# Pairs of attention heads, scan outputs and states packed side by side on the array, with later modulation products

## The chip, the cores and the metric

The kernel runs on one core of one Trainium2 chip. The metric is the device time of one execution in microseconds (us). In the profile, PE is TensorE's matmul, PEld its weight load, DVE is VectorE, ACT is ScalarE, POOL is GpSimd, SP is SyncE, which issues most of the transfers.

## What is computed

A block with two layers over 512 latent tokens of 1024 features, and 256 context tokens that only layer 0 reads. Layer 0 has one input projection; its columns feed attention (8 query heads of 64, 2 key/value heads, per-head RMSNorm, rotary positions on the latent tokens) and a bidirectional state-space scan (8 heads of 64, 2 groups, state 64, chunks of 128 tokens). Both results go through one output projection. Layer 1 is a gated short convolution. A SwiGLU feed-forward follows each layer, and shift, scale and gate vectors ("modulation") come from a conditioning vector times `ada_w`.

```python
def attend_blocks(q, keys, vals):
...
        s = jnp.einsum('bqkgd,bskd->bkgqs', qi, keys).astype(jnp.float32) * scale
        pr = jax.nn.softmax(s, axis=-1).astype(vals.dtype)
        return jnp.einsum('bkgqs,bskd->bqkgd', pr, vals)
...
    states = jnp.einsum('bclgn,bgecl,bclgep->bcgepn', bc, decay_to_end, xdt)
...
    y_off = jnp.einsum('bclgn,bgecl,cbgepn->bclgep', cc, jnp.exp(a_cs), h_in)
    y = (y_diag + y_off).reshape(b, t, nh, p)
...
        mod = (jax.nn.silu(c) @ ada_w[i] + ada_b[i])[:, None, :]
...
        x = x + g1 * m_lat
```

## The kernel before

Activations lie with features on the 128 partitions. Large projections are made of three fp32r matmuls (`mm3`: high by high, high by low, low by high part). The attention values, the scan's states and outputs and most small matmuls are plain fp32, which TensorE takes as two records each in the trace.

**Order.** Instructions are written by Python generators, and a scheduler orders each engine's queue by a simulated time line; inside `manual_schedule` PE's written order is kept. `run` calls `hybrid`, then the output projection (`project`, with a lead of three output blocks that leave out the last attention pair), the feed-forward and layer 1.

**The stretch that the change touches** is `mixer`. It projects keys, values and `dt` for six chunks, then queries, then ten blocks of features (`feature`), of which blocks 0 to 5 are convolved and 6 to 9 are the scan's gate. `heads_prep` and `rope` normalize and rotate queries and keys. The rotated query `qd` is written twice side by side (64 + 64 columns), so that one transpose of 128 columns puts the query on both halves of the partitions. `to_tok` turns features into tokens; `btok` holds each group's B twice for the same reason. `ssd_context` and `ssd` run the scan: `ssd_states` weights the tokens on POOL (`xw`) and multiplies them with the doubled B, `ssd_advance` adds the result to the running states `hin`, and `ssd_unit` (eight: four chunks by two groups) builds decay exponents (`lp`, `ep`), `cb`, and the outputs `yp`, in which one matmul of 128 weight columns covers two heads and half of the product is not used.

**Attention** goes head by head. `attn_prep` transposes the queries, finds each row's maximum with a DVE reduction over 768 scores (`mx`, line 804) and a diagonal (`dm`, line 805), and puts it into the query tile. `attn_head` makes scores (line 822), exponents on ACT (`ex`, line 824) and values (line 830): `vz` holds 64 columns of ones beside the values, so the 128 output rows are 64 values and 64 copies of the row sum. After each second head a DVE chain (lines 882 to 887) normalizes the pair.

**The interleaving** is in `mixer`: each round advances the scan one step, attention one step, and from the second round on the queue `ada` by three steps. That queue (`ada_rest`) computes three modulation vectors of layer 0 (among them the gate of the output projection): 24 loads of 256 columns by 2 through the weight ring `wst` (three buffers, shared with `take`'s prefetched weights), each followed by two DVE multiply-adds of 128 x 512 (line 257), and a transpose and reduction for each eighth product.

PSUM is dealt as three buffers of one bank (`psA`), one of one bank (`psV`), and two of two banks (`psS`).

Of the kernel before, what the change touches and what calls it, by code (L numbers as in the profile page):

```python
# [7 lines left out]
F32 = mybir.dt.float32  # L8
# [28 lines left out]
CON = {"ident": (0, 0), "ones": (0, 128), "fold": (0, 256), "pick": (0, 384), "tri_le": (1, 0), "tri_ge": (1, 128),  # L37
       "cos": (2, 0), "sin": (2, 128)}
CAT = (0, 388, 644, 900)
# [19 lines left out]
class Block:  # L59
# [328 lines left out]
    def mixer(self, mp, h, hc, hcp):  # L388
        nc, tc, t = self.nc, self.tc, self.t
        kt = [mp.tile([P, 768], F32R, name=f"kt{g}") for g in range(2)]  # L390
        vz = mp.tile([P, CHUNKS, 2, 192], F32, name="vz")
        nc.gpsimd.memset(vz, 1.0)
        dt = mp.tile([P, CHUNKS, 16], F32, name="dt")
        qd = mp.tile([P, 4, 8, 2, 64], F32, name="qd")
# [24 lines left out]
        qn = qd[:, :, :, 0, :]  # L419
        for c in range(CHUNKS):  # L420
# [5 lines left out]
            nc.vector.tensor_copy(vz[:, c, :, 64:128], kv[c][:, 128:256].rearrange("p (a b) -> p a b", a=2))  # L426
# [24 lines left out]
        btok = sm.tile([P, CHUNKS, 2, 2, 64], F32, name="btok")  # L451
# [100 lines left out]
    def rope(self, pool, dst, src, tab, nh):  # L552
# [25 lines left out]
    def to_tok(self, j, src, c0, nc_, xtok, btok):  # L578
# [8 lines left out]
        else:  # L587
            s = tp.rearrange("p c (g n) -> p c g n", g=2)
            for c in range(nc_):
                nc.scalar.copy(btok[:, c0 + c], s[:, c, :, None, :].broadcast_to([P, 2, 2, 64]))  # L590
# [54 lines left out]
    def ssd_states(self, sp, sd, c, dirs, tag):  # L645
        nc = self.nc
        out = []
        for g in range(2):
            xw = sp.tile([P, 512], F32, name="xw", tag=tag, bufs=2).rearrange("p (a b c) -> p a b c", a=2, b=4)
            st = self.psA()  # L650
            for e in dirs:
# [3 lines left out]
            lo, n = 256 * dirs[0], 256 * len(dirs)  # L655
            nc.tensor.matmul(st[:, lo:lo + n], lhsT=sd["btok"][:, c, g].rearrange("p a b -> p (a b)"),
                             rhs=xw.rearrange("p a b c -> p (a b c)")[:, lo:lo + n], start=True, stop=True)
            for e in dirs:
                r = slice(64 * e, 64 * e + 64)
                out.append((g, e, st[r, 256 * e:256 * e + 256]))  # L660
# [17 lines left out]
    def ssd_context(self, pp, sd):  # L678
# [3 lines left out]
        st0 = self.ssd_states(pp, sd, 0, (0, 1), "cs_a512")  # L682
# [6 lines left out]
        st1 = self.ssd_states(pp, sd, 1, (0, 1), "cs_a512")  # L689
# [5 lines left out]
    def ssd(self, mp, sm, m, dt, xf, zf, bf, cf, sd, feature):  # L695
# [8 lines left out]
        def advance(a, b):  # L704
            for f, t, e in ((a, a + 1, 0), (b, b - 1, 1)):
# [436 lines left out]
```

## Time and profile before

| what | value |
| --- | --- |
| median of 3 runs | 1294.94 us (1293.56 to 1295.48) |
| profiled execution | 1294.68 us |
| its span | 1292.9 us |
| PE busy | 1241.5 us, 96% |
| PE weight loads busy | 1022.4 us, 79% |
| DVE busy | 731.7 us, 57% |
| ACT busy | 448.0 us, 35% |
| POOL busy | 182.7 us, 14% |

The shares are means over the whole program. The layer projections and feed-forwards fill most of it; `mixer`'s later part lies between about 145 and 331 us of the span. A matmul's record includes the time in which its results leave the array, so records overlap and their sum is more than the time in which columns stream.

### The profile page before, as it was taken

To read this page: it belongs to the slowest core of one execution; us is meant where nothing else is said; L and a number is where in the kernel's file an instruction comes from. 1 tells how busy PE (TensorE), PEld (TensorE's weight loads), DVE (VectorE), ACT (ScalarE), POOL (GpSimd) and SP (SyncE) were. 2 spreads that over 40 slices of the span, in tenths; PEclk is the share of its full clock that TensorE was granted. 3 is DMA by queue.
4 is the path that set the end of the run, shared out by engine and by line. 5 is a ranking of instruction groups with operands and counts; after the bars stand their busy time and mean duration, and the time that the engine had idled before them with its cause. 6 is when DMAs were issued, how large, how long until landed. Compare 5 with 4: busy or idle time off the path is not lost.

```text
span 1292.9 us, 15877 instructions
## 1 busy us (share of the span) xinstructions
PE 1241.5 (96%) x6086; PEld 1022.4 (79%) x6086; DVE 731.7 (57%) x1187; ACT 448.0 (35%) x675; POOL 182.7 (14%) x199
## 2 busy tenths in 40 slices
PE   5999988899999999999999999999999999999997
PEld 3887665567798888888888988888988888888886
DVE  4898899976464777788522564443643333332223
ACT  4534534455353222222222342223532222222221
POOL 3433435440220000000000110002200000000001
PEclk9998989999999999999999999999999999999998
DMA  9331453300413777777433323333133333333322
GB/s 370 125 98 49 123 166 119 98 1 1 149 63 122 229 250 241 226 235 255 123 102 90 115 67 97 98 98 114 50 114 98 98 98 98 92 96 90 92 88 66
DMA packets 54845, 158.52 MB, mean 123 GB/s; under 512 B 6000, under 2 KB 8688, under 8 KB 54512
## 3 DMA queue, kind: packets, MB, share of 16 engines
q1 hardware_dynamic: 54480, 157.20, 38.3%
q8 instruction: 48, 0.79, 0.3%
q10 hardware_dynamic: 288, 0.31, 0.1%
q14 instruction: 29, 0.24, 0.1%
HBM read 154.86 MB, written 2.10 MB: 121 GB/s over the span
## 4 chain that ended last, share of the span: by engine, by line
PE 83%; DVE 9%; issue 3%; DMA 3%; POOL 1%; ACT 1%; SPq 0%; DVEq 0%; ACTq 0%; POOLq 0%
PE psS L116 14%; PE psS L117 14%; PE psS L118 14%; PE psA L116 10%; PE psA L118 10%; PE psA L117 10%; PE psV L830 2%; DMA adaw<-ada 2%; PE psS L961 1%; DVE xtok L257 1%; DVE mx L804 1%; PE psS L822 1%; DVE wlo L95 1%; PE psS L963 1%; DMA xT<-xT 1%
## 5 line engine op out<-in xcount | busy, mean ns | idle before, releaser
L95 DVE TENSOR_TENSOR wlo<-wst,whi 128x1024 fp32r<-128x1024 f32 (+2 forms) x194 | 234.9, 1214 | 317.2 <-ACT whi L94 311.8
L94 ACT CAST whi<-wst 128x1024 fp32r<-128x1024 f32 (+2 forms) x194 | 198.4, 1026 | 549.9 <-PE psS L117 258.5
L116 PE MATMUL psS<-act_hi,whi 128*128 128x512 f32 x760 | 297.5, 391 | 1.0 <-DVE cs_a L573 0.9
L118 PE MATMUL psS<-act_hi,wlo 128*128 128x512 f32 x760 | 297.2, 391 | 0.0
L117 PE MATMUL psS<-act_lo,whi 128*128 128x512 f32 x760 | 297.2, 391 | 0.0
L118 PEld LDWEIGHTS psS<-act_hi,wlo 128*128 128x128 f32 x760 | 143.3, 189 | 30.0
L116 PEld LDWEIGHTS psS<-act_hi,whi 128*128 128x128 f32 x760 | 143.2, 188 | 29.3 <-issue 1.2
L117 PEld LDWEIGHTS psS<-act_lo,whi 128*128 128x128 f32 x760 | 143.2, 188 | 27.7
L325 POOL TENSOR_TENSOR sq_acc<-sq_acc,sq 128x512 f32<-128x512 f32 (+1 forms) x28 | 38.0, 1356 | 872.2 <-issue 645.7
L116 PE MATMUL psA<-ffn_h_hi,whi 128*128 128x512 f32 (+1 forms) x396 | 145.4, 367 | 0.0
L117 PE MATMUL psA<-ffn_h_lo,whi 128*128 128x512 f32 (+1 forms) x396 | 145.0, 366 | 0.0
L118 PE MATMUL psA<-ffn_h_hi,wlo 128*128 128x512 f32 (+1 forms) x396 | 145.0, 366 | 0.0
L257 DVE SCALAR_TENSOR_TENSOR ada_acc<-ada_st,silu_c,ada_acc 128x512 f32<-128x512 f32 x98 | 73.5, 750 | 25.5 <-DMA ada_st<-ada 24.0
L117 PEld LDWEIGHTS psA<-ffn_h_lo,whi 128*128 128x128 f32 x396 | 74.7, 189 | 12.0
L118 PEld LDWEIGHTS psA<-ffn_h_hi,wlo 128*128 128x128 f32 x396 | 74.7, 189 | 12.1
L116 PEld LDWEIGHTS psA<-ffn_h_hi,whi 128*128 128x128 f32 x396 | 74.7, 189 | 11.9
L116 PE MATMUL psA<-act_hi,whi 128*128 128x512 f32 (+1 forms) x216 | 80.0, 370 | 0.1
L118 PE MATMUL psA<-act_hi,wlo 128*128 128x512 f32 (+1 forms) x216 | 79.2, 367 | 0.8 <-DVE wlo L95 0.8
L117 PE MATMUL psA<-act_lo,whi 128*128 128x512 f32 (+1 forms) x216 | 79.6, 368 | 0.0
L916 DVE SCALAR_TENSOR_TENSOR xT<-psA,mod,xT 128x512 f32<-128x512 f32 (+1 forms) x40 | 25.6, 643 | 67.9 <-PE psA L118 67.7
L94 ACT CAST ffn_h_hi<-sg 128x512 fp32r<-128x512 f32 x44 | 27.3, 621 | 59.0 <-DVE sg L980 59.0
L118 PEld LDWEIGHTS psA<-act_hi,wlo 128*128 128x128 f32 x216 | 40.8, 189 | 8.1 <-DVE wlo L95 1.3
(297 smaller groups left out, 1810.7 us busy)
## 6 DMA issues: line engine op xcount, KB each, us to landing
wst<-w_gu SPq DMA_DIRECT2D x88, 512.0 KB, 3.6
ada_st<-ada SPq DMA_DIRECT2D x112, 256.0 KB, 4.0
wst<-w_dn SPq DMA_DIRECT2D x32, 512.0 KB, 3.5
wst<-ada SPq DMA_DIRECT2D x24, 512.0 KB, 3.8
wst<-w_sc SPq DMA_DIRECT2D x24, 512.0 KB, 3.7
adaw<-ada SPq DMA_DIRECT2D x16, 512.0 KB, 10.4
wst<-w_dn SPq DMA_DIRECT2D x16, 384.0 KB, 3.2
wst<-w_f SPq DMA_DIRECT2D x10, 512.0 KB, 3.6
```

Of the source, the lines that this page charges most:

```text
L94: nc.scalar.copy(hi, src)
L95: nc.vector.tensor_tensor(lo, src, hi.bitcast(F32), ALU.subtract)
L116: nc.tensor.matmul(out, lhsT=a[0], rhs=b[0], start=start, stop=False)
L117: nc.tensor.matmul(out, lhsT=a[0], rhs=b[1], start=False, stop=False)
L118: nc.tensor.matmul(out, lhsT=a[1], rhs=b[0], start=False, stop=stop)
L257: nc.vector.scalar_tensor_tensor(a, w[:, i], c, a, ALU.mult, ALU.add)
L325: nc.gpsimd.tensor_tensor(self.acc[:, ts], self.acc[:, ts], sq, ALU.add)
L804: nc.vector.tensor_reduce(mx[:, c:c + 1], s[:, 0:768], AX.X, ALU.max)
L822: nc.tensor.matmul(s[:, a * T:a * T + T], lhsT=kt[x][:, ks], rhs=q[x], start=(x == 0), stop=(x == 1))
L830: nc.tensor.matmul(av, lhsT=vz[:, kc, vs], rhs=e[:, a], start=(c + a == 0), stop=(c + a == CHUNKS - 1))
L916: nc.vector.scalar_tensor_tensor(xt[:, d, ts], ps, gate[:, d:d + 1], xt[:, d, ts], ALU.mult, ALU.add)
L961: nc.tensor.matmul(out, lhsT=a[:, k * P:(k + 1) * P], rhs=hi, start=(k == 0 and a is w[0]), stop=False)
```

## The change

Attention handles two heads of a key group together. The values are multiplied with 64 weight columns for each head, one head into partitions 0 to 63 of the output and the other into 64 to 127; row sums are separate matmuls with 32 columns of ones for each head and each half of the chunk pair, into four strips of 32 partitions of a `psA` tile. The partial sums are added by one more small matmul with a new constant `pair` after the transpose. Query tiles are turned with two fp32 matmuls of 64 columns each in place of a transpose of a doubled query; `qd`, `btok` and `vz` lose their doubled or constant parts. Scan outputs and states use halves of 64 columns for two heads or two directions, and the skip term of the scan runs on 128 partitions at once. Each set of such matmuls stands in `manual_schedule`, so nothing comes between. The tiles `q1` and `q2` get four buffers and `ex` four. The `ada` queue starts in the seventh round with two steps each.

```diff
-        vz = mp.tile([P, CHUNKS, 2, 192], F32, name="vz")
-        nc.gpsimd.memset(vz, 1.0)
+        vz = mp.tile([P, CHUNKS, 2, 64], F32, name="vz")
-        qd = mp.tile([P, 4, 8, 2, 64], F32, name="qd")
+        qd = mp.tile([P, 4, 8, 64], F32, name="qd")
...
-            if rounds:
-                self.pump(3, ada)
+            if rounds > 5:
+                self.pump(2, ada)
...
-        for (u, v), o, op in zip(uv, (0, 32), (ALU.subtract, ALU.add)):
+        for i, ((u, v), o, op) in enumerate(zip(uv, (0, 32), (ALU.subtract, ALU.add))):
+            if len(dst.shape) == 3:
+                (nc.vector, nc.gpsimd)[i].tensor_tensor(dst[:, :, o:o + 32], u, v, op)
+                continue
...
-            for c in range(nc_):
-                nc.scalar.copy(btok[:, c0 + c], s[:, c, :, None, :].broadcast_to([P, 2, 2, 64]))
+            nc.scalar.copy(btok[:, c0:c0 + nc_], tp.rearrange("p c (g n) -> p c g n", g=2))
...
-            nc.tensor.matmul(st[:, lo:lo + n], lhsT=sd["btok"][:, c, g].rearrange("p a b -> p (a b)"),
-                             rhs=xw.rearrange("p a b c -> p (a b c)")[:, lo:lo + n], start=True, stop=True)
+            with self.tc.manual_schedule(engines={mybir.EngineType.PE}):
+                for c, e in ends:
+                    nc.tensor.matmul(st[64 * e:64 * e + 64], lhsT=sd["btok"][:, c, g], rhs=xw[:, e], start=True, stop=True)
...
         def advance(a, b):
+            st = self.ssd_states(sp, sd, ((2 + a, 0), (2 + b, 1)), "da")
             for f, t, e in ((a, a + 1, 0), (b, b - 1, 1)):
-                self.ssd_advance(sd, hin[t], hin[f], self.ssd_states(sp, sd, 2 + f, (e,), "da"), 2 + f, e)
+                self.ssd_advance(sd, hin[t], hin[f], st, 2 + f, e)
...
-        yp = self.psA((P, 2, 2, P))
+        yp = self.psA((P, 2, P))
+        with self.tc.manual_schedule(engines={mybir.EngineType.PE}):
+            for j in range(2):
+                for w, x, first in ((xtok[:, cc], mt, True), (hin, ce, False)):
+                    for i in range(2):
+                        at = (2 * g + j) * P + 64 * i
+                        nc.tensor.matmul(yp[64 * i:64 * i + 64, j], lhsT=w[:, at:at + 64], rhs=x[:, 2 * j + i],
+                                         start=first, stop=not first)
         for j in range(2):
...
+            pr = 2 * g + j
+            nc.vector.scalar_tensor_tensor(y[:, pr, sl], xf[:, pr, sl], self.vec("d_skip", pr, 1), yp[:, j],
+                                           ALU.mult, ALU.add)
...
-        for c in range(4):
-            nc.tensor.transpose(out=tp[:, c], in_=qd[:, c, n].rearrange("p a b -> p (a b)"), identity=self.ident)
+        with self.tc.manual_schedule(engines={mybir.EngineType.PE}):
+            for c in range(4):
+                for e in range(2):
+                    nc.tensor.matmul(tp[64 * e:64 * e + 64, c], lhsT=qd[:, c, n], rhs=self.ident, start=True, stop=True)
...
+    def attn_pair(self, ap, qs, kt, vz, u):
...
+        av, sm = self.psV(), self.psA()
...
+        def values(c):
+            e = [es.pop((h, c)) for h in range(2)]
+            first, last = c == 0, c == CHUNKS - 2
+            with self.tc.manual_schedule(engines={mybir.EngineType.PE}):
+                for a in range(2):
+                    kc = c + a + 2 if c < 4 else c + a - 4
+                    for h in (1, 0):
+                        nc.tensor.matmul(av[64 * h:64 * h + 64], lhsT=vz[:, kc], rhs=e[h][:, a], start=first and a == 0,
+                                         stop=last and a == 1)
+                for h in (1, 0):
+                    for a in range(2):
+                        r = 64 * h + 32 * a
+                        nc.tensor.matmul(sm[r:r + 32], lhsT=self.con("ones", 32), rhs=e[h][:, a], start=first, stop=last)
...
+        for c in range(0, CHUNKS, 2):
+            scores(0, c)
+            yield
+            scores(1, c)
+            yield
+            if c:
+                values(c - 2)
+                yield
+        values(CHUNKS - 2)
+        nc.scalar.copy(u[1], sm)
+        nc.scalar.copy(u[0], av)
...
+            nc.vector.transpose(flat, u[1])
+            tot = self.psA((P, 16))
+            nc.tensor.matmul(tot, lhsT=self.con("pair"), rhs=rt[:, :, 0], start=True, stop=True)
...
+            nc.vector.reciprocal(rs, tot)
```

## Rows read from the trace of the kernel before

**Rows 1.** Windows: us, then each engine's busy us (instructions), PEclk, DMA share, GB/s.

```profile
90.00:105.00 15.00, 11.90 (x57) 9.93 (x56) 15.00 (x21) 3.67 (x7) 13.36 (x14) 0.81 0.15 39
145.00:165.00 20.00, 17.07 (x66) 11.44 (x66) 19.02 (x29) 6.25 (x10) 13.27 (x15) 1.00 0.61 175
165.00:180.00 15.00, 12.31 (x40) 8.61 (x39) 13.07 (x20) 6.37 (x12) 7.25 (x11) 0.77 0.49 156
...
195.00:255.00 60.00, 50.79 (x182) 31.75 (x181) 57.75 (x86) 25.41 (x43) 31.84 (x26) 0.97 0.36 115
255.00:300.00 45.00, 41.61 (x165) 28.34 (x165) 35.12 (x71) 23.64 (x41) 15.99 (x15) 1.00 0.00 1
300.00:331.00 31.00, 31.00 (x142) 22.53 (x141) 14.01 (x28) 14.80 (x23) 0.00 (x0) 1.00 0.00 1
```

**Rows 2.** Waits, 145 to 331 us: total us, times, longest.

```profile
ACT dm L805 <- DVE mx L804: 36.5, 22, 5.9
```

**Rows 3.** Chain that ended last, 160 to 172 us: start, us, what.

```profile
162.51 3.64 DMA wst<-w_o
...
167.77 0.88 ACT dm L805 x3
```

**Rows 4.** Timeline of SyncE's queue, 138 to 190 us: start, us, instruction.

```profile
152.25 7.59 SPq L251 DMA_DIRECT2D wst<-ada  x3
```

**Rows 5.** Chain that ended last, 296 to 345 us.

```profile
297.07 0.44 PE psA L791 x4
297.51 0.43 PE psA L779 x2
...
298.38 1.72 PE psV L830 x4
...
305.22 0.92 PE psS L822 x4
...
339.21 1.23 DVE wlo L95
```

**Rows 6.** PE groups by form, 145 to 331 us: xcount, busy, mean ns.

```profile
L830 PE MATMUL psV<-ex,vz 128*128 128x512 f32 x96 | 46.8, 611 | 0.0
...
L779 PE MATMUL psA<-lx,xtok 128*128 128x256 f32 x32 | 10.1, 399 | 3.5 <-DVE xf L784 1.8 <-DVE q L795 0.9 <-DVE lx L774 0.8
L780 PE MATMUL psA<-ce,hin 128*128 128x256 f32 x32 | 9.5, 379 | 0.0
...
L656 PE MATMUL psA<-xw,btok 128*128 128x256 f32 x24 | 8.1, 447 | 0.9 <-DVE zf L479 0.5 <-POOL xw L652 0.4
...
L791 PE MATMUL psA<-cons,qd 128*128 128x128 f32 x32 | 5.2, 291 | 0.0
L656 PE MATMUL psA<-xw,btok 128*128 128x512 f32 x8 | 4.5, 641 | 2.8 <-POOL xw L652 1.8 <-ACT btok L590 1.0
```

**Rows 7.** PE timeline of `strips`, starts up to 34.19, then up to 34.40 us.

```profile
33.98 0.42 PE L203 MATMUL psS<-adaw,silu_w 128*32 128x256 f32 x4 [1.28 <-issue]
...
33.98 0.64 PE L203 MATMUL psS<-adaw,silu_w 128*32 128x256 f32 x8 [1.28 <-issue]
```

**Rows 8.** Timeline around line 761, 216.0 to 218.6 us.

```profile
216.54 0.52 PE L802 MATMUL psS<-kt,q 128*128 128x512 f32 x2
216.99 0.30 PEld L761 LDWEIGHTS psA<-cf,bf 64*128 64x128 f32 x2 [0.25 <-issue]
...
217.40 0.19 PEld L758 LDWEIGHTS psA<-da,band 128*128 128x128 f32 x1
```

**Rows 9.** DVE groups, 195 to 255 us.

```profile
L257 DVE SCALAR_TENSOR_TENSOR xtok<-wst,silu_c,xtok 128x512 f32<-128x512 f32 x20 | 22.7, 1136 | 0.3
```

**Rows 10.** DVE groups by form, 145 to 331 us.

```profile
L784 DVE SCALAR_TENSOR_TENSOR xf<-xf,vecs,psA 64x128 f32<-64x128 f32 x32 | 11.0, 343 | 10.0 <-PE psA L780 9.7
```

**Rows 11.** DVE and POOL groups by form, 80 to 106 us.

```profile
L565 DVE TENSOR_TENSOR qd<-rp_u,rp_v 128x256 f32<-128x256 f32 x8 | 4.3, 564 | 0.0
...
L565 POOL TENSOR_TENSOR qd<-rp_u,rp_v 128x256 f32<-128x256 f32 x8 | 7.8, 990 | 1.8 <-DVE rp_v L561 1.8
```

More of the change, by code (lines that the diff above doesn't have):

```diff
@@ L36 @@
 NROW = 160
-CON = {"ident": (0, 0), "ones": (0, 128), "fold": (0, 256), "pick": (0, 384), "tri_le": (1, 0), "tri_ge": (1, 128),
+CON = {"ident": (0, 0), "ones": (0, 128), "fold": (0, 256), "pick": (0, 384), "pair": (0, 388), "tri_le": (1, 0), "tri_ge": (1, 128),
        "cos": (2, 0), "sin": (2, 128)}
-CAT = (0, 388, 644, 900)
+CAT = (0, 516, 772, 1028)
 NCON = CAT[-1]
@@ L418, in mixer @@
         kn = pp.tile([P, CHUNKS, 2, 64], F32, name="kn")
-        qn = qd[:, :, :, 0, :]
+        qn = qd
         for c in range(CHUNKS):
@@ L643, in ssd_masks, with ssd_states @@
         sd.update(tri=tri, band=band)
-    def ssd_states(self, sp, sd, c, dirs, tag):
+    def ssd_states(self, sp, sd, ends, tag):
         nc = self.nc
@@ L649, in ssd_states @@
             xw = sp.tile([P, 512], F32, name="xw", tag=tag, bufs=2).rearrange("p (a b c) -> p a b c", a=2, b=4)
-            st = self.psA()
-            for e in dirs:
+            st = self.psA((P, 256))
+            for c, e in ends:
                 nc.gpsimd.tensor_tensor(
@@ L821, in scores @@
                 for x in range(2):
[L822 to L824 removed]
+                    nc.tensor.matmul(s[:, a * T:a * T + T], lhsT=kt[x][:, ks], rhs=qs[h][x], start=(x == 0), stop=(x == 1))
+            es[h, c] = ap.tile([P, 2, T], F32, name="ex", tag="ex", bufs=4)
+            nc.scalar.activation(es[h, c].rearrange("p a b -> p (a b)"), s, AF.Exp, scale=0.125)
         def values(c):
[L827 to L844 removed]
+            e = [es.pop((h, c)) for h in range(2)]
[21 more added lines that the diff above has]
+        nc.scalar.copy(u[0], av)
     def attention(self, ap, m, qd, kt, vz, ones):
@@ L852, in attention, with prep, advance @@
                                  self.con("ones")[64:128, None, :].broadcast_to([64, 6, P]), AF.Copy, scale=-1.0 / 64)
-        prep = lambda n: self.attn_prep(ap, qd, kt[n // 4][0], n, ones)
-        p = prep(0)
-        q = next(p)
-        next(p)
-        next(p)
+        def prep(n):
+            return self.attn_prep(ap, qd, kt[n // 4][0], n, ones)
+        def advance(steps):
+            for _ in range(steps):
+                while nxt and next(nxt[0], 1) is not None:
+                    nxt.pop(0)
@@ L858, in attention, with begin @@
+        def begin(p):
+            gens = [prep(2 * p + h) for h in range(2)]
+            return gens, [next(g) for g in gens]
+        nxt, qs = begin(0)
+        advance(4)
         yield
[L859 to L862 removed]
+        advance(4)
         yield
[L864 to L894 removed]
@@ new lines, in attention @@
+        advance(4)
+        for p in range(4):
+            u = [ap.tile([P, T], F32, name=x, tag=x, bufs=1) for x in ("ao", "as")]
+            pair = self.attn_pair(ap, qs, kt[p // 2], vz[:, :, p // 2], u)
+            next(pair)
+            if p < 3:
+                nxt, qn = begin(p + 1)
+            for x in range(4):
+                next(pair, None)
+                advance(1)
+                next(pair, None)
+                advance(2)
+                if x < 3:
+                    yield
+            advance(10)
+            rt = ap.tile([P, 16, 32], F32, name="rt", tag="rt", bufs=1)
+            flat = rt.rearrange("p a b -> p (a b)")
+            nc.vector.transpose(flat, u[1])
+            tot = self.psA((P, 16))
+            nc.tensor.matmul(tot, lhsT=self.con("pair"), rhs=rt[:, :, 0], start=True, stop=True)
+            rs = ap.tile([P, 16], F32, name="rs", tag="rs", bufs=1)
+            nc.vector.reciprocal(rs, tot)
+            nc.vector.tensor_copy(rt, rs[:, :, None].broadcast_to([P, 16, 32]))
+            nc.vector.transpose(u[1], flat)
+            nc.vector.tensor_tensor(u[0], u[0], u[1], ALU.mult)
+            self.split(*m.at(p), halves(u[0]))
+            qs = qn
```

88 lines of the change are left out of this document (10 added, 78 removed).

## The prediction

> **What bounds the kernel now.** I read the windows first. In most of the program TensorE is the bound, and the change touches none of that; it edits the stretch from about 90 to 331 us, so I cut only that into windows [rows 1]. What to see there is who is full. In 90 to 105 VectorE (DVE) is busy the whole 15.00 us while TensorE (PE) is busy 11.90 at a granted clock of 0.81. In 145 to 165 DVE has 19.02 of 20, in 195 to 255 it has 57.75 of 60, and PE 50.79. From 255 on the roles change: PE 41.61 of 45, then 31.00 of 31, with DVE down to 14.01. So the stage is paced by DVE up to 255 and by PE after it. The waits say how DVE passes this on: ScalarE (ACT) stood 36.5 us waiting for the row maxima of line 804 before it could write `dm` [rows 2], and the scores behind `dm` wait with it. A second kind of stop is in the chain at 162.51: a load of `w_o` that takes 3.64 us to land, and only 5 us later ACT goes on with `dm` [rows 3]. SyncE's queue shows why the load was late: modulation loads stood in it from 152.25 to 159.84, each waiting for one of the three `wst` buffers that `w_o` also needs [rows 4]. That window, 165 to 180, has PE at 12.31 of 15 and a clock of 0.77 [rows 1].
>
> **Prices.** In the PE-bound stretch the chain gives streaming times: four records of a 512-column values matmul 1.72 us, two records of a 256-column one 0.43, four query transposes 0.44, four score matmuls in fp32r 0.92 [rows 5]. A plain fp32 matmul makes two records, so it costs 0.86 at 512 columns, 0.43 at 256 and, by halving, 0.21 at 128. With the counts [rows 6]: values 96 x 0.43 = 41.3; scan outputs 64 x 0.215 = 13.8; states 24 x 0.215 + 8 x 0.43 = 8.6; transposes 32 x 0.11 = 3.5. Together 67.2 us.
>
> **Part 1, side by side.** The kernel already does this once: in `strips` four matmuls of 32 columns of weights share the array. Four records begin together and eight are over 0.22 us later than four [rows 7], the time that one 256-column record streams alone. So the strips run at full rate in parallel, and I take the same for two halves of 64. After: values 12 sets x 2 x 0.86 = 20.6, sums 12 x 0.86 = 10.3, scan outputs 8 units x 8 records x 0.107 = 6.9, states 8.6 / 2 = 4.3, the query turn, now fp32 matmuls instead of transposes, 8 heads x 8 x 0.107 = 6.9, four small totals 0.4. Sum 49.4; 17.8 us of columns go.
>
> Against that stands the switch of the array into parts and back. The nearest row is line 761, a matmul on half of the rows: the two score matmuls before it begin at 216.54 and stream 0.23 + 0.11, so the array is free at 216.88; the load begins at 216.99, and the next ordinary load at 217.40 [rows 8]. That is 0.52 us for 0.21 of columns, 0.3 lost, and the next load lies bare too; I take 0.35 a round trip. There are 12 values sets (with a second switch, 64 to 32, inside: 0.5), 8 turns, 8 output sets, 10 state sets: 12 x 0.5 + 26 x 0.35 = 15.1. Bounds: 9, if sets of the two heads or groups stand next to each other, and 20, if 64 to 32 costs a full round trip. Net on PE: **-3** (-9 to +2). The packing alone is worth little.
>
> **Part 2, modulation products.** They are 22.7 us of DVE in 195 to 255 [rows 9], 1136 ns each. Dealt from the seventh round at two a round instead of from the second at three, they leave the stretch where DVE paces. If about half of these 22.7 move past 255, DVE gets 11 us back there; PE showed 9.2 us idle (60 - 50.79), so **-8** (0, if the scheduler puts them back into the same holes, to -11). They are paid after 255, where DVE is idle 9.9 + 17.0 us [rows 1] and the work fits, but each product of 1.1 us can stand ahead of a maximum or a scan operation in DVE's queue, and PE there has no slack: **+4** (0 to +10). Their loads move too: SyncE no longer has them ahead of `w_o` at 152, so the 5 us of ACT and PE standing at 162 to 168, with the clock drop behind it, should go: **-5** (0 to -8, the clock at 0.77 for 15 us included). In exchange the third `w_o` block now waits until the last modulation load is used, near the end; its DMA of 3.64, a cast and a subtraction of 1.23 (such a subtraction is on the chain at 339.21 already [rows 5]) are covered by the projection's leading matmuls on the two blocks already there: **+1** (0 to +6 without that cover).
>
> **Part 3, less on DVE, ACT and POOL.** The skip term at line 784 was 32 instructions, 11.0 us [rows 10]; now 16 on 128 partitions, and the row's 343 ns is for the same 128 elements a partition, so 5.5 us go, about 2 of them where DVE paces: **-2** (0 to -5). The rotary result is written once instead of twice: 8 instructions on DVE of 564 ns become 4, 8 on POOL of 990 become 4 [rows 11]. They lie in 90 to 105, where DVE is full and PE loses 3.1 us and clock: **-2** (0 to -5). The `vz` memset on POOL, the copies of `btok` and the halved evacuations on ACT I cost at nothing: ACT is busy 25.41 of 60 and POOL 31.84 in 195 to 255 [rows 1]. 128 more columns of constants ride with the first loads, 0.2 us at most. The extra totals matmul lengthens each pair's normalization by about 0.5 us, covered by the next pair's scores and, for the last, by the projection's lead.
>
> **Part 4, PSUM.** The sums take one of the three `psA` buffers from the first values set of a pair to its end. The scan units (exponents, `cb`, outputs) and the preparations (queries, maxima) then share two. No row shows that; below, nothing is lost if ACT empties them in order; above, see the second rival. I take **+3**.
>
> **Sum.** -3 - 8 + 4 - 5 + 1 - 2 - 2 + 3 = -12. The profiled execution took 1294.68 us (span 1292.9, the rest around it), 0.02% under the median of 1294.94; so 1294.68 - 12 = 1282.7, say **1283**.
>
> **Rivals.**
> *The holes stay where they are (1294).* DVE's total work falls only by some 8 us, and the products also fill DVE in 145 to 165 (19.02 of 20 busy [rows 1]). If they leave that stretch idle and return where the last pairs run, the 8 and the 5 are given back there. For it: DVE is at 96% in 195 to 255. Against: 27 us of DVE are free after 255. The sum is then -3 - 2 - 2 + 4 + 3 = 0, 1294 to 1296. Chance 0.15.
> *Two buffers are not enough (1299, slower).* Eight units ask for `psA` three times each and eight preparations twice, 40 times. If each stands 0.5 us, a little more than one skip-term pair of line 784 (2 x 343 ns), less what overlaps, that is 20 us in place of 3: 1282.7 + 17 = 1300. It decides from about 0.4 us each on. For it: PE runs its queue in order, so one wait holds all. Against: ACT, which empties most of them, is under half busy. Chance 0.12.
> *Weight loads lie bare inside a set (1300, slower).* If a half's next weights could load only after its matmul, each record of a packed set would pay one load. At line 761 the two loads of 128 columns together take 0.30 and the second begins 0.11 after the first [rows 8]; per half that is about 48 + 24 + 64 + 64 + 20 = 220 records, at 0.05 to 0.11 for 64 columns: 11 to 24, so about 1300. The strips speak against it: their second group began with no gap [rows 7]. Chance 0.04. The Trainium skill ("TensorE: Matmul & The Clock Gate", Part 3, The mechanism) has a rule of this kind: a weight load overlaps a running matmul only when the row group differs, and column halves share all rows. By that rule this rival would hold; this trace disagrees, since the second group of strips followed after 0.22 us.
> *The halves don't run side by side.* Then values and sums cost 82 instead of 41: over 1320. Rows 7 exclude it for strips of 32; chance 0.02.
> *PE becomes full throughout (1270).* All idle PE time in rows 1 (3.1 + 2.9 + 2.7 + 9.2 + 3.4 = 21.3) and the half-clock spells shrink to a few us: -25. For it: the scores no longer wait for DVE; against: the order is a scheduler's. Chance 0.15.
>
> **How the numbers follow.** The forecast has 0.52, its own range 1275 to 1289. The fast case and the slow ones stand at the ends; a range of 1270 to 1297 leaves out about 2 in 10. Within 0.2% means 1292.4 to 1297.5, about what a measurement here can tell from no change. Faster: 0.52 + 0.15 + a third of the first rival, less a tail: 0.74. Same: 0.1. Slower: 0.12 + 0.04 + 0.02 less what falls short of the bound: 0.16.
>
> **What would show it.** Values records should begin in pairs, sums in fours, with 0.2 to 0.5 us lost around each set; the stretch from 145 us to the last values matmul should be about 8 to 12 us shorter; DVE in 195 to 255 should fall under 90%, and its share after 255 rise; the wait of `dm` for the maxima should drop well under 36.5; no cast should wait for `w_o` around 162. Long waits of matmuls into `psA` for line 784's successor or for the softmax copies would show the slow rival. A clock under 0.9 in new places would make the prediction wrong, as would a projection that waits for its third block.

## The result and the profile after

The changed kernel took 1307.89 us (median of 4, 1306.02 to 1308.70), the kernel before 1294.65 beside it (4 runs). The ratio is 1.0111, with a 95% interval of 1.0094 to 1.0127: 13.2 us slower, where 1283 was forecast and 1297 was the end of the range. The profiled execution took 1308.39 us, its span is 1306.6. One of the five executions of e4 below took 4328.73 us; its ratio leaves it out, and without it the median is 1299.37.

The windows of [rows 1], of the kernel after:

```profile
90.00:105.00 15.00, 14.30 (x85) 12.24 (x84) 14.75 (x24) 5.47 (x9) 9.51 (x10) 1.00 0.18 52
145.00:165.00 20.00, 15.51 (x88) 10.68 (x87) 14.85 (x21) 5.06 (x8) 4.88 (x8) 0.96 0.38 117
165.00:180.00 15.00, 10.21 (x43) 6.67 (x45) 14.66 (x22) 4.66 (x10) 5.24 (x8) 0.61 0.44 134
195.00:255.00 60.00, 47.92 (x240) 24.75 (x241) 55.13 (x79) 22.70 (x38) 23.82 (x19) 0.92 0.40 124
255.00:300.00 45.00, 38.84 (x233) 22.80 (x229) 30.12 (x48) 19.43 (x31) 20.95 (x19) 0.96 0.00 1
300.00:331.00 31.00, 29.70 (x173) 15.69 (x173) 12.67 (x31) 16.09 (x24) 2.38 (x3) 0.94 0.01 2
```

The first line is the gain that was meant: PE 14.30 where it had 11.90, at the full clock. From 145 us on, PE is less busy than in [rows 1] in every line, and the clock is below 1.00 in all five, at its lowest, 0.61 (0.77 before), in 165 to 180: there PE spends most of the time at 1.2 GHz instead of 2.4.

The PE groups by form, 145 to 331 us, as in [rows 6]:

```profile
L837 PE MATMUL psV<-ex,vz 128*64 128x512 f32 x96 | 27.4, 699 | 1.0 <-ACT ex L828 1.0
...
L842 PE MATMUL psA<-ex,cons 128*32 128x512 f32 x96 | 12.8, 605 | 0.0
...
L795 PE MATMUL psA<-cons,qd 128*64 128x128 f32 x128 | 10.2, 319 | 0.0
...
L782 PE MATMUL psA<-lx,xtok 128*64 128x128 f32 x64 | 6.9, 294 | 6.1 <-DVE lx L774 6.1
L658 PE MATMUL psA<-xw,btok 128*64 128x256 f32 x32 | 6.5, 465 | 0.0
...
L782 PE MATMUL psA<-ce,hin 128*64 128x128 f32 x64 | 6.4, 280 | 0.0
```

One packed set in PE's timeline, 292.5 to 297.5 us of the kernel after (start, us, instruction, count):

```profile
293.45 0.51 PE L806 MATMUL psS<-kt,q 128*128 128x512 f32 x2
293.89 1.94 PE L837 MATMUL psV<-ex,vz 128*64 128x512 f32 x8
295.75 1.07 PE L842 MATMUL psA<-ex,cons 128*32 128x512 f32 x8
296.75 0.97 PE L806 MATMUL psS<-kt,q 128*128 128x512 f32 x4
```

Eight values records and eight of sums hold the array from 293.79 (the maxima's two matmuls before them start at 293.45 and stream 0.34) to 296.75: 2.96 us for 1.72 + 0.86 of columns. On the array itself packing does what was priced: 0.38 us go beyond the columns, where 0.5 was taken.

To see where the time went I cut 90 to 390 us into sixty windows of 5 us and added up PE's idle time (5 less its busy time) and its clock loss (5 times what the granted clock lacks to 1.00). Idle time at the half clock counts in both, so their sum is an upper bound. "Rest" is the span less both.

| kernel | span | idle | clock loss | rest |
|---|---|---|---|---|
| before | 1292.9 | 24.3 | 8.6 | 1260.0 |
| after | 1306.6 | 34.4 | 15.4 | 1256.8 |
| after, no pairs (e3) | 1284.1 | 19.7 | 3.4 | 1261.0 |
| after, values not packed (e5) | 1296.6 | 27.0 | 10.2 | 1259.4 |
| after, sums twice (e15) | 1305.9 | 30.6 | 10.2 | 1265.1 |
| no pairs, two heads first (e18) | 1295.3 | 25.0 | 12.0 | 1258.3 |

The rest fell by 3.2 us, close to the -3 of columns and switches in the prediction. Idle time and clock loss rose by 10.1 + 6.8 us. So the question is which waits these are.

### The profile page after: what moved, and what is told of

Read it like the earlier page. It is cut to its first block, busy times and chain, and to the rows that moved or that the text cites. A ratio compares the mean times of both kernels' runs of the same rounds, so it can differ in the third digit from the quotient of the medians.

```text
span 1306.6 us, 16341 instructions
## 1 busy us (share of the span) xinstructions
PE 1242.4 (95%) x6358; PEld 1008.2 (77%) x6358; DVE 722.0 (55%) x1167; ACT 443.3 (34%) x663; POOL 170.4 (13%) x194
## 4 chain that ended last, share of the span: by engine, by line
PE 85%; DVE 10%; issue 3%; ACT 1%; POOL 1%; DMA 1%; DVEq 0%; POOLq 0%; ACTq 0%
PE psS L116 14%; PE psS L118 14%; PE psS L117 14%; PE psA L118 10%; PE psA L116 10%; PE psA L117 10%; DVE xtok L257 2%; PE psV L837 2%; PE psS L826 1%; PE psS L973 1%; DVE wlo L95 1%; DVE mx L808 1%; PE psS L203 1%; DVE lx L773 1%; PE psA L842 1%
## 5 line engine op out<-in xcount | busy, mean ns | idle before, releaser
L95 DVE TENSOR_TENSOR wlo<-wst,whi 128x1024 fp32r<-128x1024 f32 (+2 forms) x194 | 234.3, 1211 | 307.2 <-ACT whi L94 301.3
L117 PEld LDWEIGHTS psA<-act_lo,whi 128*128 128x128 f32 x216 | 40.8, 189 | 8.2 <-DVE act_lo L95 1.7
```

The lines of the kernel that those rows point to most:

```text
L95: nc.vector.tensor_tensor(lo, src, hi.bitcast(F32), ALU.subtract)
L117: nc.tensor.matmul(out, lhsT=a[0], rhs=b[1], start=False, stop=False)
```

## Experiments

First theory: one of the three `psA` buffers is held by the sums through each pair, and everything else that needs one waits. Its rivals: the order of the pairs (both heads are prepared before either is scored, and a set waits for both); the packed form itself; the dealing of the products. Lines named below are those of the changed kernel; in a variant they can lie a few lines off.

**Which part costs.** Three kernels take parts back out of the changed one, one keeps the queries alone.

```diff
  e3: attn_pair, attention, vz, two q1/q2 buffers as before the change
-            if rounds > 5:
-                self.pump(2, ada)
+            if rounds:                  # e4; e7 = e3 + e4
+                self.pump(3, ada)
  e8: e7 with ssd_states, advance, yp and btok as before, too
```

> The changed kernel with attention head by head as before (values with 64 columns of ones, no sums tile, two buffers for exponents); queries, scan and dealing stay changed. Theories 'buffer' and 'pairs': 1295 us or less, perhaps 1288 with the rotary and scan gains. Theory 'dealing': 1303 or more.

> The changed kernel with the products dealt from the second round at three a round, as before. Theory 'dealing': 1298 us or less. Theories 'buffer' and 'pairs': 1304 to 1310, with only the fold of the products earlier than 333 us.

> Only the once-written queries and the packed scan outputs and states are kept; attention per head and the dealing of the modulation products are as before the change. With pairs the new dealing cost 1307.9 - 1299.5 = 8 us. If that cost is the dealing's own: 1286.4 - 8 = 1278. If it is there only because of the pairs' late gaps: 1285 to 1288. If the new dealing helps once attention goes per head (the 8 us of the prediction): 1291 to 1295.

> Only the once-written queries and their turn by eight fp32 matmuls remain of the change; scan, attention and dealing are as before it. The feature stage ended 4 us earlier in the changed kernel. If that lead lasts to the end: 1289 to 1291. If the stage behind it is paced by VectorE and takes the lead back: 1293 to 1296. If the eight turns with their switches (8 x 0.35, columns doubled) cost more than they give: 1296 to 1299.

| kernel | us | ratio to before (95%) |
|---|---|---|
| e8, queries only | 1292.03 | 0.9984 (0.9975 to 0.9994) |
| e7, and scan packed | 1287.05 | 0.9943 (0.9928 to 0.9958) |
| e3, and new dealing | 1286.41 | 0.9956 (0.9941 to 0.9971) |
| e4, queries, scan and pairs, dealing as before | 1299.45 | 1.0053 (1.0032 to 1.0074) |
| after, all four | 1307.89 | 1.0111 (1.0094 to 1.0127) |

The queries gain 2.2 us against the 1294.2 that ran beside them (between two of the expected ranges), the packed scan 5.0 more. The dealing does nothing by itself (1287.05 against 1286.41) and costs 8.4 with pairs. The pairs, that is order and packed values together, cost 12.4 us with the old dealing, 21.5 with the new. Without them (e3, e7) the change beats the kernel before by 0.4 to 0.6%.

**The held buffer.** e1 takes the sums' buffer away, e2 gives the old kernel one that is held through each pair of heads.

```diff
-        av, sm = self.psV(), self.psA()                  # e1
+        av = self.psV()
...
+                        nc.tensor.matmul(av[r:r + 32], lhsT=self.con("ones", 32), rhs=e[h][:, a], start=True, stop=True)
...
+            if n % 2 == 0:                               # e2
+                held = self.psA()
+                nc.tensor.matmul(held[:, 0:1], lhsT=self.con("ones"), rhs=self.con("ones", 1), start=True, stop=False)
```

> The sums are written into the bank of the values instead of a psA tile of their own (same matmuls, each started afresh; the softmax denominator is left out, a constant 1 stands for it). Theory 'buffer' (the sums hold one of three psA buffers, so the scan, the fold of the modulation products and the projection's lead come late): 1297 us or less, the first lead matmul of the projection before 325 us. Theory 'dealing' (the later rounds of the products are at fault) and theory 'pairs' (the switches of the array and the waits for two heads' exponents are at fault): 1304 to 1309, since neither is touched.

> The kernel before, with one psA buffer held from the first values of a pair to its end by a one-column matmul and released by a one-column copy. Theory 'buffer': 1303 us or more, scan and projection late as in the changed kernel. Theories 'dealing' and 'pairs': 1294 to 1297, the price of eight tiny matmuls.

e1 gave 1304.11 (1303.90 to 1305.89), 3.8 of the 13 us back, with the first matmul of the projection at 329.9 us. That is far from the 1297 of the theory. In the old kernel the held buffer cost about 10 us (1304.02, ratio 1.0069, 1.0043 to 1.0094), as the theory had it, but its runs lie apart (two of ten at 1293.9, one at 1298.4, seven between 1303.9 and 1305.3), and its profile has the clock at 0.73 in 225 to 240 and 0.77 in 300 to 315, where the kernel before has 1.00. So a held buffer can cost that much in the old order; in the changed kernel it isn't the main cause, and some 4 us of it stay.

**Packed form or order.** e5 keeps the order of pairs and its two buffers per pair, with ordinary values matmuls; e9 is e5 with each set kept together; e15 adds columns to the changed kernel.

```diff
-                        nc.tensor.matmul(av[64 * h:64 * h + 64], lhsT=vz[:, kc], rhs=e[h][:, a], start=first and a == 0,
+                    nc.tensor.matmul((av, sm)[h], lhsT=vz[0][:, kc].rearrange("p a b -> p (a b)"), rhs=e[h][:, a],   # e5
...
+            with self.tc.manual_schedule(engines={mybir.EngineType.PE}):                                          # e9
...
+                for h in (1, 0):                                                                                   # e15
+                    for a in range(2):
+                        r = 64 * h + 32 * a
+                        nc.tensor.matmul(sm[r:r + 32], lhsT=self.con("ones", 32), rhs=e[h][:, a], start=False, stop=last)
```

> The changed kernel with its order of heads by pairs and its two buffers per pair, but each head's values as ordinary 128-column matmuls (the weights are the values of both key groups) into a buffer of its own; the sums are left out and a constant 1 stands for the softmax denominator. Columns go from 12 x 2.56 = 30.7 us to 96 x 0.43 = 41.3, and 12 switches of 0.5 go: +4.6 us if TensorE's columns set the time. Theory A, the order (values wait for two heads, all preparation of a pair stands ahead of its first scores, the gaps are waits): 1303 to 1312, the gaps stay where they are, and 165 to 180 us again has a granted clock near 0.6. Theory B, the packed sets themselves cost far more than 0.5 us each (bare loads, drains): 1288 to 1298.

> As the run with ordinary 128-column values in the order of pairs (1298.6), which also leaves out the sums and has a constant 1 for the denominator, but the four values matmuls of a set are kept together on TensorE, so a set starts only when the exponents of both heads are there and nothing stands between its matmuls. Theory C, keeping a set together costs (TensorE has nothing to put into the waits): most of the 9.3 us between 1298.6 and the 1307.9 of the changed kernel come back, 1303 to 1309. Theory B, the packed form costs (switches, narrow loads): 1296 to 1300, no change.

> The changed kernel with the four sums matmuls of every set issued twice in the same kept set (the denominator doubles): 12 x 0.86 = 10.3 us more columns on TensorE and no other work. If TensorE's columns set the time of the stage: +8 to +11, 1316 to 1319. If the columns fall into time that TensorE has idle anyway, or hold its clock up: 1303 to 1311. That tells what the 10 to 18 us of columns saved by packing could have been worth.

e5 took 1298.64 (1298.12 to 1299.00), e9 1299.06 (1298.05 to 1300.48). Keeping a set together costs nothing here. e5 falls between its two expectations: the order costs 12.2 us against e3, and the packed form 9.3 more, although it has fewer columns. The held buffer of e1 belongs to the 12.2 and not to the 9.3, since e5 holds a `psA` buffer through each pair as well. What makes the 9.3 is not settled.

e15 took 1308.67 (1307.64 to 1313.21), 0.8 more for 10.3 us of columns. Its windows:

```profile
165.00:180.00 15.00, 11.36 (x51) 7.58 (x53) 14.61 (x22) 5.13 (x10) 5.24 (x8) 0.51 0.45 138
195.00:255.00 60.00, 50.58 (x290) 26.52 (x290) 53.18 (x80) 23.50 (x39) 23.91 (x20) 0.97 0.39 123
255.00:300.00 45.00, 38.87 (x248) 21.59 (x248) 29.51 (x46) 19.32 (x33) 21.90 (x20) 1.00 0.00 1
```

In the table above its rest is 8.3 us larger and its idle time and clock loss 9.0 smaller than those of the kernel after: the columns went into idle time, and the clock of 195 to 255 rose from 0.92 to 0.97. By the ratios beside their own kernels before, e15 is 2 us above the kernel after, within the intervals of both. In this order TensorE's columns have next to no price. That saving them has no worth is argued from it; e5, with more columns and 9.3 us faster, agrees. e15 also has the clock loss of e5 again (10.2 us each, 15.4 after), so a part of the 9.3 may be clock; no run separates it.

**VectorE's work, or the loads behind it.** The products with 32 of 512 columns (e10 with pairs, e11 without), and the same with their loads cut as well (e13, e14). A load brings the weights of two products, 512 columns each.

```diff
-                            nc.vector.scalar_tensor_tensor(a, w[:, i], c, a, ALU.mult, ALU.add)
+                            v = slice(0, 32 if acc is not None else 512)
+                            nc.vector.scalar_tensor_tensor(a[:, v], w[:, i, v], c, a[:, v], ALU.mult, ALU.add)
...
+                    nc.sync.dma_start(out=w[:, :, v], in_=t["ada"][layer, part * 2 + j, :, k:k + step, v])   # e13, e14
```

> The changed kernel with each modulation product of the mixer taken over 32 of its 512 columns (the rest of the modulation is left out; loads, count of instructions and order stay): some 35 us of VectorE go out of 145 to 345 us. Theory A1, VectorE's load turns the pairs' waits into a loss: together with the next run, the pairs cost under 8 us more than no pairs, and this run is 1275 to 1285. Theory A2, the chain of two heads itself (maxima, diagonal, scores, exponents, one set) costs whatever VectorE has to do: still 14 to 22 us more than no pairs, 1288 to 1298.

> Attention per head (1286.4) with the same shortened products (the rest of the modulation is left out). TensorE's idle time and clock loss from 90 to 390 us were 19.0 + 3.4 us there; if VectorE's load makes them, some 8 to 12 us go: 1274 to 1279. If they are waits of other kinds: 1283 to 1286. The difference to the run before this one tells A1 (under 8) from A2 (14 to 22).

> The changed kernel with the mixer's modulation products and their loads both over 32 of 512 columns (the rest of the modulation is left out): each of the 24 loads is a sixteenth of its bytes, so no product stands in VectorE's queue waiting for its load with maxima behind it. Theory L, the loads of the products hold the maxima of the pairs: TensorE's idle time and clock loss from 145 to 200 us fall from 16.9 to under 8, and with the next run the pairs cost under 10 us; this run 1284 to 1292. Theory O, the order of the pairs makes its gaps by itself: 14 to 22 us above the next run, 1296 to 1305.

> Attention per head (1286.4) with the same light products and loads (the rest of the modulation is left out). If the loads pace the stage here too: 1275 to 1282. If not: 1284 to 1288, as with the shortened products alone (1287.3). The difference of the run before this one to it tells theory L (under 10) from theory O (14 to 22).

e10 took 1304.49, e11 1287.32, both slower than any of their expected ranges: 17.2 us between them, and without pairs no gain at all (1286.41 with the whole products). VectorE in 195 to 255 us, of e10, then of e11:

```profile
195.00:255.00 60.00, 52.73 (x286) 29.00 (x283) 44.13 (x79) 27.26 (x45) 25.71 (x22) 0.94 0.32 101
```

```profile
195.00:255.00 60.00, 55.06 (x271) 34.12 (x269) 41.20 (x81) 29.95 (x50) 28.38 (x27) 0.97 0.25 80
```

DVE is down to 44.13 from the 55.13 of the kernel after, and to 41.20 from 56.94 in e3, and the time doesn't follow. What the products do hold up is seen in DVE's timeline of e10:

```profile
161.06 0.54 DVE L258 SCALAR_TENSOR_TENSOR xtok<-wst,silu_c,xtok 128x32 f32<-128x32 f32 x2 [2.29 <-DMA wst<-ada]
161.52 0.95 DVE L809 TENSOR_REDUCE mx<-psS 128x1 f32<-128x768 f32 x1
```

A product stands in DVE's queue and waits 2.29 us for its load; the maximum stands behind it. With light loads e13 took 1299.01 (ratio 1.0040, 1.0023 to 1.0057) and e14 1282.77 (0.9920, 0.9905 to 0.9934): the lighter loads give 5.5 us against e10 and 4.6 against e11, about the same with pairs and without, and 16.2 us between the two remain. In e13 the idle time and clock loss of 145 to 200 us is 12.3 us, down from 16.9, not under 8. The pairs, order and packed form together, make most of their gaps without the products and their loads.

**The start of the first pair.** e18 gives attention per head the pairs' start and nothing else; e6 moves the first head's scores forward; e17 and e16 move the scan forward; e12 joins e1, e4 and e6.

```diff
         qn = next(nxt)
+        for _ in nxt:          # e18, on e3: head 1's maxima before head 0's scores
+            pass
         yield
...
         nxt, qs = begin(0)     # e6
-        advance(4)
+        advance(2)
         yield
-        advance(4)
+        advance(3)
         yield
-        advance(4)
...
             next(pair)
+            advance(10)        # e6: head 0's scores, then head 1's maxima
...
             alive = next(s, 1) is None
+            if rounds in (1, 2):            # e17; e16: rounds in (4, 6, 8, 10)
+                alive = (next(s, 1) is None) or alive
```

> The changed kernel, but the first pair's scores of head 0 follow right after head 0's own four maxima, and head 1's four maxima come behind them; the other pairs as they are. Theory A with the start as its dearest place: the clock of 165 to 180 us returns from 0.61 to over 0.9, and the time is 1298 to 1303. Theory A with the loss spread over all four pairs: 1304 to 1308. Theory B: 1306 to 1309, no change.

> The changed kernel with three edits at once that were each tried alone: dealing as before (-8.4), the first pair's head 0 scored before head 1's maxima (-3.7), the sums put into the values' buffer so that no buffer is held (-3.8; it leaves out the denominator, a constant 1 stands in its place, and the accumulation of values). If the three are separate losses: 1292, still above the 1286 to 1287 without pairs, and the rest of 5 is the kept sets. If they are one loss seen three times (TensorE without cover in 150 to 255 us): 1296 to 1299. If pairs are sound once these are eased: 1282 to 1286.

> The changed kernel with the scan given two steps instead of one in four rounds (the fifth, seventh, ninth and eleventh), so that its last output and the gate come earlier against attention. In the changed kernel the last skip term starts at 312.4 (298.8 before) and no projection matmul runs before 333. If the late scan is what the pairs cost at the end (no leading projection matmuls under the last pair): the last skip term back under 300 and 1294 to 1300. If the time is lost before 255 us and the end only shows it: 1304 to 1309.

> The changed kernel with the scan given two steps in the second and third rounds, so that its second state step and the projections of its features (the matmuls of lines 116 to 118 that cover attention per head at 168 to 175) stand under the eight maxima of the first pair. In the changed kernel the first exponent matmul of the scan (line 757) starts at 206.9, against 199.6 before the change, and the last skip term at 312.4 against 298.8. If the start of the first pair is what delays the scan, and the scan the end: first exponent matmul under 200, TensorE's idle time plus clock loss in 145 to 200 us from 16.9 to under 9, and 1293 to 1300. If every pair makes its own gaps: 1303 to 1310.

> Attention per head (1286.4, idle time plus clock loss of 7.0 in 145 to 200 us), with one edit: the second head's four maxima are taken before the first head's first scores, as the pairs do at their start; all behind it goes per head as before. If this start is most of what the order of pairs costs (12 us with ordinary values): 1294 to 1299, with the clock of 165 to 180 us near 0.6. If it is a small part, as the 3.7 us that the first head ahead gave back: 1288 to 1291. If it costs nothing: 1285 to 1287.

e18 took 1297.11 (1296.53 to 1298.32), 10.7 us above e3: this start by itself costs nearly as much as the 12.2 of the order in e5. PE's timeline of e3, without pairs (line 807 makes scores for maxima, 813 the diagonal product, 827 scores, 659 the scan's states, 835 values, 116 to 118 a feature projection):

```profile
157.23 1.03 PE L807 MATMUL psS<-kt,q 128*128 128x512 f32 x4
160.47 0.50 PE L827 MATMUL psS<-q,kt 128*128 128x512 f32 x1 [2.21 <-DVE mx L809]
161.76 0.50 PE L813 MATMUL psA<-dm,tri 128*128 128x512 f32 x1 [0.80 <-ACT dm L810]
...
163.12 1.88 PE L659 MATMUL psA<-xw,btok 128*64 128x256 f32 x8
...
166.91 1.08 PE L659 MATMUL psA<-xw,btok 128*64 128x256 f32 x8
...
168.38 1.88 PE L835 MATMUL psV<-ex,vz 128*128 128x512 f32 x4
169.70 0.79 PE L116 MATMUL psA<-act_hi,whi 128*128 128x512 f32 x1
```

The same stretch of e18:

```profile
161.93 0.70 PE L813 MATMUL psA<-dm,tri 128*128 128x512 f32 x1 [3.92 <-ACT dm L810]
...
165.21 1.65 PE L807 MATMUL psS<-kt,q 128*128 128x512 f32 x4 [0.69 <-ACT q L799]
167.78 1.87 PE L807 MATMUL psS<-kt,q 128*128 128x512 f32 x4 [0.92 <-DVE mx L809]
170.17 0.79 PE L827 MATMUL psS<-q,kt 128*128 128x512 f32 x1 [0.52 <-DVE mx L809]
...
174.31 1.76 PE L659 MATMUL psA<-xw,btok 128*64 128x256 f32 x8
```

And of the kernel after:

```profile
158.89 0.40 PE L118 MATMUL psA<-act_hi,wlo 128*128 128x512 f32 x1
161.42 0.62 PE L806 MATMUL psS<-kt,q 128*128 128x512 f32 x2 [2.13 <-DVE mx L808]
...
165.63 0.98 PE L806 MATMUL psS<-kt,q 128*128 128x512 f32 x2 [2.75 <-DVE mx L808]
...
168.37 1.98 PE L658 MATMUL psA<-xw,btok 128*64 128x256 f32 x8
170.27 0.97 PE L806 MATMUL psS<-kt,q 128*128 128x512 f32 x4
175.00 0.80 PE L826 MATMUL psS<-q,kt 128*128 128x512 f32 x1 [3.76 <-DVE mx L808]
```

Per head, four maxima pass, then scores, two state steps (163.12, 166.91) and the projection of the next features follow at once. With both heads first, eight maxima stand in a row: PE waits for their reductions on DVE and has little to put between, and its clock is 0.64 (e18) and 0.61 (after) in 165 to 180 us, where e3 has 0.95. The windows of e3, then of e18:

```profile
165.00:180.00 15.00, 14.14 (x56) 9.46 (x55) 14.45 (x23) 3.46 (x5) 10.06 (x15) 0.95 0.46 150
```

```profile
165.00:180.00 15.00, 13.35 (x36) 7.77 (x37) 14.61 (x23) 5.40 (x9) 4.18 (x7) 0.64 0.64 199
```

Idle time and clock loss, by stretch, say how much of the pairs' loss is made there:

| idle + clock loss, us | 145 to 200 | 200 to 255 | 255 to 335 |
|---|---|---|---|
| e3 | 5.3 + 1.7 | 7.1 + 1.7 | 4.4 + 0.0 |
| e18 | 9.2 + 7.0 | 7.9 + 5.0 | 4.2 + 0.0 |
| e5 | 9.5 + 6.9 | 6.9 + 3.4 | 6.8 + 0.0 |
| after | 10.0 + 6.9 | 11.3 + 4.8 | 8.2 + 3.7 |

In 145 to 200 e18, e5 and the kernel after lose the same, 9 to 10 us more than e3. In e5 that is 9.4 of the 14.1 that it has above e3 from 90 to 390 us. What the packed form adds to e5 lies behind the start, 5.8 us in 200 to 255 and 5.1 in 255 to 335.

The scan's first state step in this stretch starts at 174.31 (e18) or 168.37 (after) instead of 163.12, and everything of the scan comes later:

| start in us of | before | after | e3 | e18 | e17 |
|---|---|---|---|---|---|
| the scan's first exponent matmul (751) | 199.6 | 206.9 | 191.2 | 201.9 | 190.6 |
| the last skip term (786) | 298.8 | 312.4 | 285.5 | 297.2 | 289.2 |
| the last values matmul | 329.9 | 329.3 | 320.8 | 332.5 | 326.5 |
| the first leading projection matmul (116) | 316.5 | 334.0 | 307.2 | 319.0 | 330.1 |

The last line shows where the delay comes out: before the change the output projection began 13 us ahead of the last values matmul, after it 5 us behind. In e18 it still begins 13.5 ahead, and the loss shows as a last values matmul 11.7 us later than in e3. With pairs this lead is lost in all twelve kernels, e5 among them: the projection starts 3.5 to 4.7 us after the last values matmul, and in the eight kernels without pairs 13.0 to 13.6 ahead of it.

e17, the scan early, took 1301.27 (1299.68 to 1303.40): the first exponent matmul comes at 190.6 and 6.6 us are back, the middle between its two expectations; idle time and clock loss in 145 to 200 us are 11.8 (under 9 was expected). e6 took 1304.17, 3.7 back, in the range of a loss spread over all four pairs. But it did not mend the start: its clock in 165 to 180 us is 0.62 and not over 0.9, and its idle time and clock loss in 145 to 200 us are 16.3. So it leaves open what the start is worth in the changed kernel. e12, with the three gains of 8.4, 3.7 and 3.8 together, took 1303.32, above all its ranges and more than e4 alone (1299.45): they don't add, and the single figures depend on how the scheduler deals the rest. e16, the scan pushed forward in the middle, took 1318.43 (ratio 1.0190, 1.0172 to 1.0209), slower than all it was expected to be: the last skip term comes at 299.7, but the last values matmul at 343.7. The lead's last input from attention, on DVE, and its first matmul, on PE:

```profile
334.90 0.69 DVE L95 TENSOR_TENSOR act_lo<-ao,act_hi 128x512 fp32r<-128x512 f32 x1 [2.54 <-ACT act_hi L94]
```

```profile
347.24 0.48 PE L116 MATMUL psA<-act_hi,whi 128*128 128x512 f32 x1
```

That input is the third pair's; the gate's features were split at 327.8 already. So the activations that the lead reads were there over 11 us before its first matmul. An earlier scan by itself doesn't bring the lead back; what else holds it behind the last pair was not tested.

## Why the prediction was wrong

**The step that failed** is the order, which the sum prices at nothing. Its parts count columns, switches, products and buffers; that the pairs put head 1's four maxima ahead of head 0's scores, the scan's state step and the next features' projection has no term. It cost 10.7 us alone (e18), and 12.2 in the pairs (e5) together with the held buffer, for which part 4 had 3. A second step failed beside it: part 1 took columns saved for time saved. By its own figures the packed values were worth 4.4 us (41.3 less 30.9 of columns, 6 for switches); they cost 9.3 (e5 against the kernel after), and why stays open. Of the 25 us between 1282.7 and 1307.9 the first step makes about 9 (12.2 less 3), the second about 14 (9.3 and the 4.4).

**"So the stage is paced by DVE up to 255"** read a busy share as a bound. 57.75 of 60 is right, but with the products a sixteenth as wide it is 41 to 44, and the time is 3.4 us less with pairs (e10) and 0.9 more without (e11). Both are variants of the changed kernel; no run shortens the products in the kernel before. 11 to 16 of DVE's us in this window were work that the pace doesn't hang on. What sets the pace instead is argued from e18 and the waits: the chain of maxima, diagonal, scores and exponents, and what PE has to do meanwhile.

**Part 1, -3:** right as time on the array (-3.2 in the rest), wrong as time of the kernel. The switches are near the price: the set above has 0.4 us beyond its columns, 0.5 was taken. But in this order 10.3 us of added columns cost 0.8 (e15).

**Part 2, -8, +4, -5, +1:** the lower bound of the first came true, "0, if the scheduler puts them back into the same holes". The groups of DVE in 195 to 255 us of the kernel after, to be held against [rows 9], and SyncE's queue, against [rows 4]:

```profile
L257 DVE SCALAR_TENSOR_TENSOR xtok<-wst,silu_c,xtok 128x512 f32<-128x512 f32 x22 | 21.3, 967 | 0.2
```

```profile
142.48 47.44 SPq L251 DMA_DIRECT2D wst<-ada  x13
```

The products and their loads are where they were, in the order of the scheduler's time line rather than of the dealing. With pairs the new dealing cost 8.4 us (e4), without them nothing (e3, e7). No load of `w_o` stands among them at 162 any more, but the maxima stop PE there, and the clock of 165 to 180 fell further, so the -5 is not to be seen. The third block did no harm: the longest wait of the projection is 1.4 us, for the low part of its activations.

**Part 3, -2 and -2:** the mechanism is right. 16 skip terms take 4.8 us in this stretch where 32 took 11.0 [rows 10]; the stretch from 90 to 105 is at the full clock, and e8 is 2.2 us faster than before. e8 also holds the turns of the queries, which part 1 charges with 3.4 us of columns and 2.8 of switches: again columns did not cost their price.

**Part 4, +3:** near in size (3.8, e1), though the old kernel paid about 10 for a held buffer (e2).

**The rivals.** The slow side came true by another mechanism than "Two buffers are not enough", whose 20 us are 3.8 in e1. "The holes stay where they are" was right of the products. "Weight loads lie bare inside a set" is excluded: the eight values records above last 1.86 us to the first sum, for 1.72 of columns, so the halves run side by side and their loads are hidden. PEld's records of the set start while those matmuls run:

```profile
293.88 0.20 PEld L837 LDWEIGHTS psV<-ex,vz 128*64 128x64 f32 x4 [0.25 <-issue]
294.37 0.14 PEld L837 LDWEIGHTS psV<-ex,vz 128*64 128x64 f32 x2 [0.28 <-issue]
```

The rule of the Trainium skill ("TensorE: Matmul & The Clock Gate", Part 3, The mechanism) by which only another row group lets a load overlap disagrees with this trace, as it did with the strips; the same section also lets a load into a background weight buffer go ahead, which the trace doesn't contradict. One sum of the prediction doesn't come out: its terms for "faster" make 0.72 before the tail is taken off, not 0.74.

**What was to be seen.** Values in pairs and sums in fours came. The wait of `dm` for the maxima is 30.0 us (36.5 in [rows 2]), not "well under":

```profile
ACT dm L809 <- DVE mx L808: 30.0, 22, 5.9
```

DVE in 195 to 255 is 92% (55.13 of 60), not under 90, its share after 255 fell instead of rising (30.12 and 12.67 us, from 35.12 and 14.01), and the stretch to the last values matmul is 0.6 us shorter, not 8 to 12. "A clock under 0.9 in new places would make the prediction wrong" came true. Three windows of the kernel after where the kernel before has 1.00:

```profile
205.00:210.00 5.00, 3.56 (x12) 1.75 (x14) 4.85 (x7) 1.47 (x3) 0.00 (x0) 0.78 0.46 152
280.00:285.00 5.00, 5.00 (x38) 3.00 (x35) 3.15 (x8) 0.83 (x2) 0.00 (x0) 0.71 0.01 3
315.00:320.00 5.00, 5.00 (x21) 2.27 (x21) 1.49 (x3) 3.09 (x5) 0.00 (x0) 0.70 0.00 0
```

## What to carry to other kernels

Before taking work off an engine, add some to it in the same stretch: if the time hardly moves (here 0.8 us for 10.3 of columns), a saving there is worth little either. When units of work are joined in pairs, list what the second unit's preparation now stands ahead of, and look for what is left to cover its waits; the first pair, before the pipeline is full, was the dearest stretch here. A share of busy time alone names no bound: cut that work in the stretch and see whether the time follows.

## What the runs showed of the hardware

VectorE's scaling of the decay (line 773) took 367 ns on average before the change and 511 after, for the same 128 elements. It goes with POOL's work beside it. DVE's timeline of the kernel after, then POOL's:

```profile
224.11 3.48 DVE L773 SCALAR_TENSOR_TENSOR lx<-lx,dt 128x128 f32<-128x128 f32 x4
```

```profile
223.97 1.12 POOL L755 TENSOR_TENSOR da<-cons,dta_hi 128x512 fp32r<-128x512 f32 x1 [0.99 <-PE psA L758]
225.04 1.08 POOL L755 TENSOR_TENSOR da<-cons,dta_lo 128x512 fp32r<-128x512 f32 x1
226.09 1.08 POOL L770 TENSOR_TENSOR lx<-lx,dt 128x512 f32<-128x512 f32 x1
```

Four instructions take 870 ns each while POOL runs three of 1.1 us. Of the 32 records of the kernel after, 21 with POOL idle for at least half of them have a mean of 340 ns, 11 with POOL beside them 838; before the change it was 26 of 342 and 6 of 476. The Trainium skill ("SBUF — State Buffer", Who interferes with whom) says that a VectorE instruction with two SBUF inputs and a GpSimd instruction that reads SBUF can't run together, and the later one waits; these numbers agree. The maxima, which read PSUM, stay at 950 ns in both kernels. No run here prices this; it is 4.7 us of VectorE's time.
